# Where the rows lie in on-chip memory: token and key rows of a hybrid decoder layer alternate between two places modulo 256 bytes

## The chip, the core and the metric

The kernel runs on one core of one Trainium2 chip. A core has a matrix engine (TensorE; PE in the profile, with its weight loads listed apart as PEld), a vector engine (DVE), an activation engine (ACT), a general engine (POOL), a queue engine (SP), sixteen DMA engines, and an on-chip memory of 128 partitions that all engines read. Only TensorE multiplies matrices; its results go to accumulator banks that DVE and ACT read. The metric is the device time of one execution in microseconds (us). Differences of 0.2% (3 us here) are about what the runs can tell apart.

## The reference: what is computed

One layer of a decoder for 4,096 new tokens of one sequence and 64 tokens of eight others, model width 1,024, in float32:

```python
h = _rmsnorm(x, g_pre)
z = h @ w_in                                   # 1024 -> 2816 columns
cb, cc, ch, cg, q, k, v, ag, mq, mg = _split_cols(z)
out_a = silu(cg) * cb * conv3(cc * ch)         # gated convolution, 256 channels
out_b = silu(ag) * _window_prompt(q, k, v, sink)   # 8 heads, window 128
out_c = silu(mg) * _mem_attend(mq, mk, mv)     # 4 heads over 256 memory tokens
y = concat(out_a, out_b, out_c) @ w_out        # 1024 -> 1024
return x + _rmsnorm(y, g_post)
```

The keys and values of the memory tokens come from one more small projection of the memory rows.

## The kernel before

**Precision.** TensorE takes float32 operands in a one-pass form (`F32R` in the code) that keeps only the upper part of a number. Where that isn't enough an operand is split into `hi` (what the form keeps) and `lo` (the rest), and a product is the sum of three: weight hi by token hi, weight hi by token lo, weight lo by token hi. So most matmuls come in threes.

**Input projection** (`product`, the matmul at L373). Tokens go in 8 blocks of 520, a block as two halves of 260 columns. Blocks of weights and tokens are multiplied by Strassen's scheme in Winograd's form: seven products instead of eight (`PRODUCTS`), in three phases over groups of output columns (`PHASES`); the first two blocks of the first phase use the eight plain products. A product for one 128-wide group of outputs is twelve matmuls of 128x260: four slices k of the contraction, and for each the three of the split. The tokens stream through TensorE (the *moving* operand: row k of `hi` or `lo`, 260 numbers in each partition) against a loaded *stationary* operand (128 numbers in each partition, from a weight slot `w`, hi at `w[:, 0]` and lo at `w[:, 1]`). The order in a three is: hi against w-hi, lo against w-hi, hi against w-lo. There are 2x8x4x12 + (6x7x4 + 8x7x4 + 8x7x3)x12 = 7,488 such matmuls. `split` writes `hi` on ACT (L363) and `lo` on DVE (L364) one product ahead; DVE adds the results into the z tiles (L380).

**Attention and output projection.** Then, for each block of 128 tokens, 48 matmuls at L1499 (line `TE.matmul(acc, self.hl[l][:, k], wo[k]...)` in `Block.run`): 8 slices k, two halves of 512 columns, threes again. Here the 512 output weights `wo` are the moving operand, and the split attention result `mh` (hi) and `ml` (lo) the stationary one. 30 blocks run all 48 so with 512 columns, one more 24 (and 48 of 256 columns instead of the other 24), the block of the 64 sampled tokens 32 with a tile `mh_s`: 1,512 matmuls of 512 columns with `mh` or `ml`, and 32 with `mh_s`. Between them stand the matmuls of attention for a later chunk of 256 tokens: scores of the window (L1253, moving keys `kst`, hi part then lo part, against stationary queries `q`; 512 of 256 columns), scores of the memory (L1189, moving memory keys `mk` against `q`; 256 of 256 columns), transposes (L1204, L1276, L1153, moving the unit matrix) and the float32 sums with the values (L1095, L1225, L1231). `Block.split` makes `mh` on ACT (L1479) and `ml` on DVE (L1480).

**What sets the order.** In the plain blocks and the first phase the order on every engine is the program's. Later a list scheduler orders each engine's instructions by its own estimates, under the dependencies and the buffers: a tile of a pool can only be written when the pool's buffer is free again. The addresses come from the pools: these are laid out one behind the other on the left and right side of a partition, each as large as its tiles, so a pool that grows moves all behind it.

**Places.** The lines that set them: `wa = tile_pool(name="wa", bufs=3 * NP_)` (21 slots of 4,096 bytes: weights in the projection, then `wo`, `mh`, `ml` and the gain of the last norm), `wb` with 7 more, `hp` with two buffers for each of `hi` and `lo`, rows of `XR = 320` numbers (1,280 bytes) of which 260 are used, starting at number 48 (`hi`) or 16 (`lo`).

Of the kernel before, what the change touches and what calls it, by code (L numbers as in the profile page):

```python
# [8 lines left out]
F32 = mybir.dt.float32  # L9
F32R = mybir.dt.float32r  # L10
# [5 lines left out]
P = 128  # L16
D = 1024
KT = D // P
KH = KT // 2
# [2 lines left out]
NB = 8  # L22
NT = 4096 + NS
HW = 260
XR = 320
NBLK = NT // (2 * HW)
CT = 256
NCH = 4096 // CT
# [13 lines left out]
NP_ = len(PRODUCTS)  # L42
# [10 lines left out]
def hybrid_layer(ctx: ExitStack, tc: tile.TileContext, a: dict):  # L53
# [27 lines left out]

    wa = ctx.enter_context(tc.tile_pool(name="wa", bufs=3 * NP_))
    pa = ExitStack()
    wb_stack = ExitStack()
    wb = wb_stack.enter_context(tc.tile_pool(name="wb", bufs=NP_, side="right"))
# [1 line left out]

    place = ctx.enter_context(tc.tile_pool(name="place", bufs=1)).tile([P, 2, KH, HW], F32, name="place")  # L90
    hxp = pa.enter_context(tc.tile_pool(name="hx", bufs=4))
    hp = pa.enter_context(tc.tile_pool(name="hp", bufs=2))
    own = ExitStack()
    kept_z = ExitStack()
    zp, used = {}, {1: [], 2: []}
# [75 lines left out]
        return tp.tile([P, wide + 2 * HW], F32, tag="t", name=name)  # L171

    def w_slot(qi, name):
        return (wa if qi < 3 else wb).tile([P, 2, 512], F32R, tag="w", name=name)

    def w_raw(pair, o):

# [66 lines left out]
    nat, sq, after_nat = {}, [0], [14]  # L244
# [7 lines left out]
    def row_load(j):  # L252
        if j < 5 * NBLK:
            g = RG * j - NS
            if 2 <= j < 10 or 12 <= j < 14:
                t = (wa if j < 7 or j == 12 else wb).tile([P, 2, 512], F32, tag="w", name=f"nat{j}")
                t = nat[j] = t.rearrange("p a n -> p (a n)")
            else:
                t = nat[j] = natp.tile([P, D], F32, tag="nat", name=f"nat{j}")
            if g < 0:  # L260
                DMA.dma_start(t[:NS], a["x_s"])
                DMA.dma_start(t[NS:RG], a["x_p"][: RG - NS, :])
            else:
                DMA.dma_start(t[:RG], a["x_p"][g : g + RG, :])
# [86 lines left out]
                tc.keep_in_program_order(ins)  # L351
            store(hd[b][o], ops[o])

    begins = {"hi": 48, "lo": 16}

    def split_tile(tag, name):

        n = begins[tag]
        return hp.tile([P, KH, XR], F32R, tag=tag, name=name)[:, :, n : n + HW]

    def split(src, name):
        hi, lo = split_tile("hi", f"hi{name}"), split_tile("lo", f"lo{name}")
# [340 lines left out]
    x_of(0, 0, "B21")  # L703

    idle = accumulator(1, 2, "idle")
    warm = hp.tile([P, KH, XR], F32R, tag="lo", name="warm").rearrange("p k n -> p (k n)")
    G.memset(f(warm[:, : P + 512]), 1.0)
    for n in (416, 416, 416, 416, 512, 512, 512, 416):
        TE.matmul(idle[:, 0, :n], warm[:, :P], warm[:, P : P + n], start=True, stop=True)
# [19 lines left out]
    third = {}  # L729

    def third_start():
        keep = right.enter_context(tc.tile_pool(name="memkv", bufs=1, side="right"))
        third["mk"] = keep.tile([P, 2, 4, 256], F32R, name="mk")
        third["mkv"] = keep.tile([P, 2, 512], F32, name="mkv")

        third["vt"] = keep.tile([P, P], F32, name="vt")
        sink, nsink = (keep.tile([P, 8], F32, name=n) for n in ("sink", "nsink"))
        third["sink"], third["nsink"] = sink, nsink
        wmask = third["wmask"] = keep.tile([P, 2, P], U8, name="wmask")
        negs = third["negs"] = keep.tile([P, 2, P], F32, name="negs")  # L740
# [8 lines left out]
        third["mrows"] = third["pre"].tile([P, 4, P + CT], F32, tag="k", name="mrows").rearrange("p a n -> p (a n)")  # L749
# [262 lines left out]
    def open_attention():  # L1012

        nonlocal ps, mixp, places, vp, bp, bq, yp
        own.close()
        mem_stack.close()
        psa.close()
        pa.close()

        ps = {tag: ctx.enter_context(tc.tile_pool(name=f"ps{tag}", bufs=1 if tag == "pv" else 2, space=bass.MemoryType.PSUM))  # L1020
              for tag in ("s", "t", "z", "pv")}
        vp = ctx.enter_context(tc.tile_pool(name="vp", bufs=5, side="right"))
        yp = ctx.enter_context(tc.tile_pool(name="yp", bufs=2, side="right"))
# [12 lines left out]
        DMA.dma_start(third["scol"][:, 0:1], a["sinkcol"])  # L1036
# [60 lines left out]
    class Chunk:  # L1097
# [10 lines left out]
        def load_keys(self):  # L1108
            c, t0 = self.c, self.t0

            self.kst = self.pool("k").tile([P, 4, P + CT], F32R, tag="k", name=f"kst{c}")
            lo = P if c == 0 else 0
            if c == 0:
                G.memset(f(self.kst[:, :, 0:P]), 0.0)
            for kvh in range(2):
                for half in range(2):
                    G.dma_start(self.kst[half * 64 : half * 64 + 64, 2 * kvh : 2 * kvh + 2, lo:],  # L1117
                                  qd[:, 0, kvh * 64 : kvh * 64 + 64, t0 - P + lo : t0 + CT].rearrange("a p n -> p a n"))
            self.vT = self.pool("vT").tile([P, CT], F32, tag="vT", name=f"vT{c}")
            DMA.dma_start(self.vT, vd[:, self.ts])  # L1120
# [252 lines left out]

    def sample_window():
        zs = third["zs"]
        keys = bp["k"].tile([P, 4, P + CT], F32, tag="k", name="skc").rearrange("p a n -> p (a n)")
# [15 lines left out]
        values = third["pre"].tile([P, 4, P + CT], F32, tag="k", name="svc").rearrange("p a n -> p (a n)")  # L1392
# [63 lines left out]
    class Block:  # L1456
# [233 lines left out]
```

## Time and profile before

| what | value |
|---|---|
| median of 3 runs | 1530.43 us (1530.04 to 1531.11) |
| the profiled execution | 1529.03 us, of which 1527.3 us are the span from the first to the last instruction |
| TensorE (PE) busy | 1514.2 us, 99% of the span, 11,331 matmuls |
| weight loads (PEld) busy | 1391.6 us, 91% |
| DVE, ACT, POOL busy | 1145.1, 806.2, 381.0 us |
| granted TensorE clock | 1.000 of full speed |

Times in the profile's views are us from the span's start. A group's row has line, engine, operation, result<-operands, shape and count; then the time busy, the mean of one in ns, and the idle time before them. A matmul's duration reaches from its first column to its last result, so neighbours overlap, and what one matmul costs the engine is read from the distance between starts: in the timeline the first column is a row's start, the second its length, and `x2` says that two alike stand in it. The names of tiles are shortened: `hi_6T` is a `hi` tile, `w_2S` a weight slot, and digits that only number buffers are left out.

### The profile page before, as it was taken

The page shows a single profiled execution, that of the slowest core. Times are in us where ns is not written, and L with a number is a line of the kernel's source. Part 1 is how long each engine was busy: PE and PEld are TensorE (multiplying, and loading weights), DVE is VectorE, ACT ScalarE, POOL GpSimd, SP SyncE. Part 2 cuts the span into 40 slices and gives each one's busy share as a digit, 9 for nine tenths or more (in the row PEclk, how much of TensorE's full clock was granted, in tenths as well). Part 3 has the DMA queues.
Part 4 walks back from the last instruction along what each step waited for, and adds up shares of the span by engine and source line. Part 5 has one row for each costly group of instructions (what it writes and reads, how often), then busy time and mean ns, then how long its engine had stood idle before and what let it go on. Part 6 is the DMA issues. An engine that isn't in the chain of part 4 may idle for free.

```text
span 1527.3 us, 30150 instructions
## 1 busy us (share of the span) xinstructions
PE 1514.2 (99%) x11331; PEld 1391.6 (91%) x11331; DVE 1145.1 (75%) x2055; ACT 806.2 (53%) x2039; POOL 381.0 (25%) x604
## 2 busy tenths in 40 slices
PE   9999999999999999999999999999999999999998
PEld 9999999999999999999999998788888888888876
DVE  6778888899887777997677678766666666666743
ACT  7776666576222222445455457656655565565632
POOL 0222333221300000000101204544444444444310
PEclk9999999999999999999999999999999999999999
DMA  9989999878755333778877789977777777776333
GB/s 274 200 213 242 286 277 259 301 238 273 194 182 181 127 127 127 240 231 278 243 262 224 242 286 259 226 160 149 149 148 152 162 149 158 162 155 145 131 110 97
DMA packets 177943, 306.28 MB, mean 201 GB/s; under 512 B 33926, under 2 KB 107654, under 8 KB 177766
## 3 DMA queue, kind: packets, MB, share of 16 engines
q1 hardware_dynamic: 130901, 227.38, 48.2%
q0 software_dynamic: 46176, 75.92, 24.9%
q8 instruction: 90, 1.47, 0.4%
q10 hardware_dynamic: 720, 1.05, 0.2%
q14 instruction: 56, 0.45, 0.1%
HBM read 197.23 MB, written 108.05 MB: 200 GB/s over the span
## 4 chain that ended last, share of the span: by engine, by line
PE 87%; DVE 5%; issue 4%; DMA 2%; POOL 1%; ACT 1%; SPq 0%; ACTq 0%; POOLq 0%; DVEq 0%
PE c L373 47%; PE y L1499 23%; PE ws L1253 4%; PE wo L1095 2%; PE wt L1276 2%; PE xs L1189 2%; PE xt L1204 2%; PE wo L1225 2%; PE wo L1231 1%; PE mem_acc L796 1%; DVE z L380 1%; DMA ws10A<-in_w_in 1%; DMA vd<-v 1%; DMA place<-hd_B 0%; DMA ws20A<-in_w_in 0%
## 5 line engine op out<-in xcount | busy, mean ns | idle before, releaser
L1499 PE MATMUL y<-wo,mh 128*128 128x512 f32 (+1 forms) x1040 | 350.1, 399 | 0.0
L380 DVE TENSOR_TENSOR z<-c,z 128x520 f32<-128x520 f32 (+1 forms) x308 | 194.8, 647 | 80.7 <-PE c L373 79.0
L1499 PEld LDWEIGHTS y<-wo,mh 128*128 128x128 f32 x1040 | 194.3, 188 | 39.3 <-issue 2.4
L1499 PE MATMUL y<-wo,ml 128*128 128x512 f32 (+1 forms) x520 | 201.8, 388 | 0.0
L1266 ACT ACTIVATE sm<-sm,wnm 128x128 f32<-128x128 f32 x256 | 99.5, 390 | 60.9 <-DVE wnm L1260 60.0
L1198 POOL TENSOR_SCALAR xp<-xp,xrd 128x256 f32<-128x256 f32 x128 | 74.6, 590 | 208.0 <-DVE xrd L1194 207.1
L1499 PEld LDWEIGHTS y<-wo,ml 128*128 128x128 f32 x520 | 98.2, 189 | 16.2
L1190 DVE TENSOR_REDUCE xmx<-xs 128x2 f32<-128x512 f32 x64 | 44.1, 689 | 59.3 <-PE xs L1189 59.2
L1278 ACT COPY wpt<-wt 128x512 f32<-128x512 f32 x64 | 37.2, 582 | 87.7 <-PE wt L1276 85.2
L1253 PEld LDWEIGHTS ws<-kst,q 128*128 128x128 f32 x512 | 70.0, 190 | 5.4 <-ACT xp L1193 0.7
L1506 DVE TENSOR_TENSOR yn<-y,gpost 128x512 f32<-128x512 f32 (+1 forms) x66 | 45.1, 684 | 39.6 <-PE y L1499 39.3
L1253 PE MATMUL ws<-kst,q 128*128 128x256 f32 x512 | 73.1, 283 | 0.4 <-ACT xp L1193 0.4
L1507 ACT ACTIVATE y<-y 128x512 f32<-128x512 f32 (+1 forms) x66 | 38.5, 584 | 64.2 <-DVE yn L1506 64.2
L744 POOL CAST wmask<-negs 128x256 uint8<-128x256 f32 x1 | 0.8, 822 | 265.2 <-ACT z L382 265.2
L1286 POOL TENSOR_SCALAR_AFFINE_SELECT wpt<-wpt 128x512 f32<-128x512 f32 x64 | 52.7, 823 | 42.0 <-ACT wpt L1278 39.1
L1193 ACT ACTIVATE xp<-xs,xnm 128x256 f32<-128x256 f32 x128 | 58.9, 464 | 7.1 <-DVE xnm L1191 7.1
L1128 POOL DMA_DIRECT2D q<-qd x64 | 42.8, 674 | 70.2 <-DMA qd<-zh 60.2
L1117 POOL DMA_DIRECT2D kst<-qd x64 | 38.7, 617 | 63.7 <-PE xt L1204 41.5
L1517 DVE SCALAR_TENSOR_TENSOR xr<-yn,yst,xr 128x1024 f32<-128x1024 f32 (+2 forms) x34 | 43.1, 1269 | 14.6 <-POOL yst L1513 13.2
L1256 DVE COPY_PREDICATED sm<-wmask,ws 128x256 f32<-128x256 uint8 x124 | 52.1, 436 | 2.4 <-ACT sm L1255 2.0
L1283 POOL TENSOR_SCALAR_AFFINE_SELECT wpv<-wpt 128x512 f32<-128x512 f32 x62 | 40.5, 653 | 50.6 <-ACT wpt L1278 50.5
L275 ACT ACTIVATE nat<-nat 104x1024 f32<-104x1024 f32 x40 | 42.3, 1057 | 18.5 <-DMA nat<-in_x_p 18.5
(962 smaller groups left out, 5076.2 us busy)
## 6 DMA issues: line engine op xcount, KB each, us to landing
q<-qd POOLq DMA_DIRECT2D x64, 384.0 KB, 8.3
xr<-in_x_p SPq DMA_DIRECT2D x32, 512.0 KB
nat<-in_x_p SPq DMA_DIRECT2D x39, 416.0 KB
o_yp<-xr SPq DMA_DIRECT2D x31, 512.0 KB
md<-th POOLq DMA_DIRECT2D x48, 260.0 KB, 7.2
qd<-zh SPq DMA_DIRECT2D x48, 260.0 KB
qd<-z SPq DMA_DIRECT2D x48, 260.0 KB
kst<-qd POOLq DMA_DIRECT2D x60, 192.0 KB, 5.5
```

Source lines behind the costliest of these rows:

```text
L373: TE.matmul(bank[:, :HW], l, r, start=first and i == 0, stop=last and i == 3 * KH - 1)
L380: add = lambda dst, other: V.tensor_tensor(dst, c, other, op=ALU.add)
L1190: V.tensor_reduce(mx[:, :nb], s, axis=AX.X, op=ALU.max)
L1193: S.activation(p[:, i, :], s[:, i, :], AF.Exp, bias=nm[:, i : i + 1], scale=SCALE, accum_out=den[:, i : i + 1])
L1198: G.tensor_scalar(p[:, i, :], p[:, i, :], rd[:, i : i + 1], 0.5, op0=ALU.mult, op1=ALU.mult)
L1253: TE.matmul(s3[:, hh, :], self.q[:, 4 + 2 * (2 * half + hh) + kvh, i * P : i * P + P], self.kst[:, 2 * kvh + part, i * P : i * P + 2 * P], ...
L1256: V.copy_predicated(sm[:, 2 * half : 2 * half + 2, :], third["wmask"], third["negs"] if first else s3[:, :, 0:P])
L1266: S.activation(sm[:, hh, :], sm[:, hh, :], AF.Exp, bias=nm[:, hh : hh + 1], scale=SCALE, accum_out=den[:, hh : hh + 1])
L1286: G.affine_select(p3, p3, pattern=[[0, 4], [1, P]], compare_op=ALU.is_ge, fill=0.0, base=0, channel_multiplier=-1)
L1499: TE.matmul(acc, self.hl[l][:, k], wo[k][c0 // 512][:, r, c0 % 512 : c0 % 512 + c1 - c0], start=j == 0, stop=j == passes * KT - 1)
L1506: V.tensor_tensor(yn[:m, c0:c1], acc[:m], gpost[:m, c0:c1], op=ALU.mult)
L1517: V.scalar_tensor_tensor(self.xr[:m, cs], yn[:m, cs], st[:m, 3:4], self.xr[:m, cs], op0=ALU.mult, op1=ALU.add)
```

## The change

No instruction is added or removed: each engine has the same instructions as before. What changes is where tiles lie in a partition. Unused tiles (`pad`) are put between pools, rows get other lengths, `hi` and `lo` get a pool each, and four of the 21 slots of `wa` become a pool `wm` of their own, which holds four of the 28 weights of a phase (S3 of the column groups 0 and 1, A22 of 1 and 2) and later `mh` and `ml`. As the pools lay it out, the starts of the operands modulo 256 bytes are:

| operand | before | after |
|---|---|---|
| `hi`, row k, moving in L373 | 32 | 32 for even k, 160 for odd k (rows of 288 numbers) |
| `lo`, row k, moving in L373 | 160 | 160 for even k, 32 for odd k |
| weights, stationary in L373 | 224 | 224; 160 in the four slots of `wm` |
| `wo`, moving in L1499 | 224 | 224 |
| `mh`, `ml`, stationary in L1499 | 224 | 160 |
| `mh_s`, stationary in L1499 (sampled tokens) | 96 | 160 |
| `kst`, moving in L1253 | 96 or 160, hi and lo part alike | 160 hi part, 32 lo part (rows of 416 numbers) |
| `q`, stationary in L1253 and L1189 | the same place as `kst` | 96 |
| `mk`, moving in L1189 | 160, hi and lo part alike | 160 hi part, 32 lo part |
| unit matrix / what is transposed | 160 / 96 or 160 | 160 / 96 |
| float32 sums: moving / stationary | 96 / 160 | L1095 160 / 160, L1225 and L1231 96 / 96 |

"Moving minus stationary" below is the moving operand's place less the place of the stationary one that is loaded for the next matmul while it streams, modulo 256. It goes, in L373, from 64 for `hi` and 192 for `lo` to 64 and 192 by turns for either, so that the moving rows of successive matmuls lie at 32, 160, 32, 160 without a break (before: 32, 160, 32, 32, 160, 32); where the loaded weights lie in `wm`, to 128 and 0 by turns. In L1499 it goes from 0 to 64, in L1253 from 0 to 64 (hi part) and 192 (lo part).

The core of the diff:

```diff
-XR = 320
+XR = 288
+KR = 416
...
+    def pad(where, n):
+        pads[0] += 1
+        where.enter_context(tc.tile_pool(name=f"pad{pads[0]}", bufs=1)).tile([P, n], F32, name=f"pad{pads[0]}")
...
-    wa = ctx.enter_context(tc.tile_pool(name="wa", bufs=3 * NP_))
+    wa = ctx.enter_context(tc.tile_pool(name="wa", bufs=3 * NP_ - 4))
+    pad(ctx, 48)
+    wm = ctx.enter_context(tc.tile_pool(name="wm", bufs=4))
...
-    hp = pa.enter_context(tc.tile_pool(name="hp", bufs=2))
+    pad(pa, 32)
+    hp = {"lo": pa.enter_context(tc.tile_pool(name="hplo", bufs=2))}
+    pad(pa, 32)
+    hp["hi"] = pa.enter_context(tc.tile_pool(name="hphi", bufs=2))
...
     def w_slot(qi, name):
-        return (wa if qi < 3 else wb).tile([P, 2, 512], F32R, tag="w", name=name)
+        o = name[name.index("_") + 2 :]
+        pool = wm if (o, qi) in (("S3", 0), ("S3", 1), ("A22", 1), ("A22", 2)) else wa if qi < 3 else wb
+        return pool.tile([P, 2, 512], F32R, tag="w", name=name)
...
-    begins = {"hi": 48, "lo": 16}
-
     def split_tile(tag, name):
-        n = begins[tag]
-        return hp.tile([P, KH, XR], F32R, tag=tag, name=name)[:, :, n : n + HW]
+        return hp[tag].tile([P, KH, XR], F32R, tag=tag, name=name)[:, :, :HW]
...
-        third["mk"] = keep.tile([P, 2, 4, 256], F32R, name="mk")
+        third["mk"] = keep.tile([P, 2, 4 * 256 + 32], F32R, name="mk")[:, :, : 4 * 256].rearrange("p a (h k) -> p a h k", k=256)
...
+        pad(att, 16)
         bq = att.enter_context(tc.tile_pool(name="bq", bufs=1))
...
+        pad(att, 16)
         keys = att.enter_context(tc.tile_pool(name="keys", bufs=1))
...
-            self.kst = self.pool("k").tile([P, 4, P + CT], F32R, tag="k", name=f"kst{c}")
+            self.kst = self.pool("k").tile([P, 4, KR], F32R, tag="k", name=f"kst{c}")[:, :, : P + CT]
...
-            parts = lambda n: wa.tile([P, 2, 512], F32R, tag="w", name=n).rearrange("p a (b n) -> p (a b) n", n=P)
+            parts = lambda n: wm.tile([P, 2, 512], F32R, tag="w", name=n).rearrange("p a (b n) -> p (a b) n", n=P)
```

Since the slots of `wm` come free at other times than those of `wa` did, the scheduler's order differs at the seam between the projection and the output projection and for some blocks behind it; the order within L373 is the same throughout. Two places show it. On ACT, in the last products of the projection, the split of the output weights (`wo`, L181 before, L196 after), of the tokens (`hi`, L363 and L375) and of the first block's attention result (`mh`, L1479 and L1494). Before:

```order
L181 CAST wo_0_11673<-wor_11586 128x512
L363 CAST hi_7B_11710<-x_7B_11588 128x4x260
L181 CAST wo_0_11727<-wor_11645 128x512
L181 CAST wo_0_11730<-wor_11647 128x512
L181 CAST wo_0_11747<-wor_11649 128x512
L1479 CAST mh_11772<-place 128x1024
L363 CAST hi_7T_11776<-x_7T_11651 128x4x260
```

After:

```order
L196 CAST wo_0_11692<-wor_11605 128x512
L1494 CAST mh_11791<-place 128x1024
L375 CAST hi_7B_11729<-x_7B_11607 128x4x260
L196 CAST wo_0_11746<-wor_11664 128x512
L196 CAST wo_0_11749<-wor_11666 128x512
L196 CAST wo_0_11766<-wor_11668 128x512
L375 CAST hi_7T_11795<-x_7T_11670 128x4x260
```

The `mh` of block 0 moves ahead of one `hi` and three `wo`. On PE, in the second half of block 0's output projection (`y_1`), the scores of a window (`ws`, L1253 and L1268) of chunk 1. Before:

```order
L1499 MATMUL y_1_12155<-wo_1_11806,mh_11772 128x512
L1499 MATMUL y_1_12155<-wo_1_11806,ml_11773 128x512
L1499 MATMUL y_1_12155<-wo_1_11806,mh_11772 128x512
L1499 MATMUL y_1_12155<-wo_1_11823,mh_11772 128x512
L1499 MATMUL y_1_12155<-wo_1_11823,ml_11773 128x512
L1499 MATMUL y_1_12155<-wo_1_11823,mh_11772 128x512
L1253 MATMUL ws_1_0_12053<-kst_11254,q_11261 128x256 x4
L1253 MATMUL ws_1_1_12060<-kst_11254,q_11261 128x256 x4
```

After:

```order
L1514 MATMUL y_1_12185<-wo_1_11825,mh_11791 128x512
L1514 MATMUL y_1_12185<-wo_1_11825,ml_11792 128x512
L1268 MATMUL ws_1_0_12083<-kst_11273,q_11280 128x256 x4
L1268 MATMUL ws_1_1_12090<-kst_11273,q_11280 128x256 x4
L1514 MATMUL y_1_12185<-wo_1_11825,mh_11791 128x512
L1514 MATMUL y_1_12185<-wo_1_11842,mh_11791 128x512
```

The eight matmuls of the scores now stand behind two of the 24 of `y_1` instead of behind six.

More of the change, by code (lines that the diff above doesn't have):

```diff
@@ L79, in hybrid_layer @@
     md = tc.dram_tile([KT, P, NT], F32, name="md")
-    wa = ctx.enter_context(tc.tile_pool(name="wa", bufs=3 * NP_))
+    pads = [0]
+    def pad(where, n):
[4 more added lines that the diff above has]
+    wm = ctx.enter_context(tc.tile_pool(name="wm", bufs=4))
     pa = ExitStack()
@@ L255, in row_load @@
             if 2 <= j < 10 or 12 <= j < 14:
-                t = (wa if j < 7 or j == 12 else wb).tile([P, 2, 512], F32, tag="w", name=f"nat{j}")
+                t = (wm if j == 3 else wa if j < 7 or j == 12 else wb).tile([P, 2, 512], F32, tag="w", name=f"nat{j}")
                 t = nat[j] = t.rearrange("p a n -> p (a n)")
@@ L705, in hybrid_layer @@
     idle = accumulator(1, 2, "idle")
-    warm = hp.tile([P, KH, XR], F32R, tag="lo", name="warm").rearrange("p k n -> p (k n)")
+    warm = hp["lo"].tile([P, KH, XR], F32R, tag="lo", name="warm").rearrange("p k n -> p (k n)")
     G.memset(f(warm[:, : P + 512]), 1.0)
@@ L748, in third_start @@
         third["parts"] = third["pre"].tile([P, 12, CT], F32, tag="q", name="mparts").rearrange("p (a b) n -> p a (b n)", a=6)
-        third["mrows"] = third["pre"].tile([P, 4, P + CT], F32, tag="k", name="mrows").rearrange("p a n -> p (a n)")
+        third["pre"].tile([P, 16], F32, tag="pad", name="padk")
+        third["mrows"] = third["pre"].tile([P, 4, KR], F32, tag="k", name="mrows").rearrange("p a n -> p (a n)")
         third["mem"] = mem_stack.enter_context(tc.tile_pool(name="mem", bufs=3, side="right"))
@@ L1375, in sample_window @@
         zs = third["zs"]
-        keys = bp["k"].tile([P, 4, P + CT], F32, tag="k", name="skc").rearrange("p a n -> p (a n)")
+        keys = bp["k"].tile([P, 4, KR], F32, tag="k", name="skc").rearrange("p a n -> p (a n)")[:, : 4 * (P + CT)]
         kc = keys[:, : NB * P].rearrange("p (b k) -> p b k", b=NB)
@@ L1391, in sample_window @@
         yield
-        values = third["pre"].tile([P, 4, P + CT], F32, tag="k", name="svc").rearrange("p a n -> p (a n)")
+        values = third["pre"].tile([P, 4, KR], F32, tag="k", name="svc").rearrange("p a n -> p (a n)")[:, : 4 * (P + CT)]
         vc = values[:, : NB * P].rearrange("p (b k) -> p b k", b=NB)
```

## The prediction

> **What bounds the kernel.** I read the page first: busy shares, granted clock, chain.
>
> ```profile
> PE 1514.2 (99%) x11331; PEld 1391.6 (91%) x11331; DVE 1145.1 (75%) x2055; ACT 806.2 (53%) x2039; POOL 381.0 (25%) x604
> PEclk9999999999999999999999999999999999999999
> PE 87%; DVE 5%; issue 4%; DMA 2%; POOL 1%; ACT 1%; SPq 0%; ACTq 0%; POOLq 0%; DVEq 0%
> PE c L373 47%; PE y L1499 23%; PE ws L1253 4%; PE wo L1095 2%; PE wt L1276 2%; PE xs L1189 2%; PE xt L1204 2%; PE wo L1225 2%; PE wo L1231 1%; PE mem_acc L796 1%; DVE z L380 1%; DMA ws10A<-in_w_in 1%; DMA vd<-v 1%; DMA place<-hd_B 0%; DMA ws20A<-in_w_in 0%
> ```
>
> TensorE is busy in all 40 slices at its full clock, and 70% of the chain are two lines: the input projection (L373) and the output projection (L1499). Then the waits of PE, to see whether anything holds it:
>
> ```profile
> PE idle L709 <- POOL warm L707: 2.2, 1, 2.2
> PE c L373 <- DVE lo_2T L364: 0.9, 2, 0.5
> ```
>
> These are the two longest: nothing to gain there. No matmul is taken away either, so the change can only act on the pace at which matmuls follow each other. The pace comes from stretches in which PE does one thing only. First L373 in the stretch from 600 to 700 us, then its single starts in the timeline:
>
> ```profile
> 600.00:700.00 100.00, 100.00 (x851) 100.00 (x850) 1.00 0.72 239
> ```
>
> ```profile
> 600.01 0.28 PE L373 MATMUL c<-lo_6T,w_3S 128*128 128x260 f32 x1
> 600.13 0.40 PE L373 MATMUL c<-hi_6T,w_3S 128*128 128x260 f32 x2
> 600.37 0.28 PE L373 MATMUL c<-lo_6T,w_3S 128*128 128x260 f32 x1
> 600.48 0.40 PE L373 MATMUL c<-hi_6T,w_3S 128*128 128x260 f32 x2
> 600.72 0.28 PE L373 MATMUL c<-lo_6T,w_3S 128*128 128x260 f32 x1
> 600.84 0.40 PE L373 MATMUL c<-hi_6T,w_3S 128*128 128x260 f32 x2
> ...
> 602.13 0.28 PE L373 MATMUL c<-lo_6T,w_0S 128*128 128x260 f32 x1
> ```
>
> (851 overlap the stretch, some two of them only at its edges: 100 us / 849 = 117.8 ns.) From 600.01 to 602.13 stand six threes: 2.12 us / 6 = 353.3 ns, 117.8 each. Within a three the distances are unequal: after a `lo` 0.12, 0.11, 0.12 us, so 116 to 117; I take 116, which leaves (353.3 - 116) / 2 = 118.6 for a `hi`. Columns, stationary size and engine are the same, so something about `lo` is 2.6 ns cheaper. What differs by the table of places is that `lo` moves from 160 and `hi` from 32, 192 and 64 above the weights. The start of the kernel shows a second pace at the same places:
>
> ```profile
> 8.70 0.28 PE L373 MATMUL c<-lo_0B,w_1A 128*128 128x260 f32 x1
> ...
> 11.22 0.28 PE L373 MATMUL c<-lo_0B,w_3A 128*128 128x260 f32 x1
> ...
> 11.62 0.28 PE L373 MATMUL c<-lo_0B,w_3A 128*128 128x260 f32 x1
> ...
> 13.74 0.28 PE L373 MATMUL c<-lo_0B,w_0A 128*128 128x260 f32 x1
> ```
>
> Seven threes in 2.52 us are 360 ns each (120 a matmul); behind a short interruption at 11.3 six take 2.12 again. So the pace is one of several patterns that hold themselves. The output projection has the same: unsettled behind other matmuls, settled after some ten of its own.
>
> ```profile
> 1107.79 0.40 PE L1499 MATMUL y<-wo,ml 128*128 128x512 f32 x1
> ...
> 1110.11 0.40 PE L1499 MATMUL y<-wo,mh 128*128 128x512 f32 x1
> 1110.34 1.12 PE L1253 MATMUL ws<-kst,q 128*128 128x256 f32 x8
> 1111.30 0.60 PE L1204 MATMUL xt<-ident,xp 128*128 128x128 f32 x4
> ...
> 1495.00 0.39 PE L1499 MATMUL y<-wo,ml 128*128 128x512 f32 x1
> ...
> 1501.80 0.39 PE L1499 MATMUL y<-wo,ml 128*128 128x512 f32 x1
> ```
>
> The eleven from 1107.79 to 1110.34 take 231.8 ns each, the thirty from 1495.00 to 1501.80 take 226.7. The eight scores at 1110.34 take 120.0. One row shows L1499 at another place, 128 above its stationary operand, for the sampled tokens:
>
> ```profile
> L1499 PE MATMUL y<-wo,mh_s x32: 390/392/404, 1502.3 to 1509.5; 128*128 128x512 f32 x32
> ```
>
> 31 distances in 7.2 us are 232.3 ns, and it doesn't settle though nothing interrupts it. The settled sums have a common measure: 226.7, 120.0, 353.3 and 360 ns are 34, 18, 53 and 54 times 6.67 ns. I use that below as a guess at which paces can hold.
>
> **The change part by part.** The span's own execution took 1529.03 us, 1.4 below the median; the terms are differences to it and go to the median unchanged.
>
> *Product rows by turns.* 28 weights a phase, four in `wm`: S3 and A22 in two column groups are 2x2x12 matmuls in each of 22 Winograd blocks, A22 in two groups used twice in the two plain ones: 1,056 + 96 = 1,152. The other 6,336 keep weights at 224 while their rows go from two at 32 and one at 160 to half and half. At the two rows' prices a pair takes 118.6 + 116 = 234.6, 117.3 each: -0.5 ns, -2.9 us. If only multiples of 6.67 hold, the nearest pair is 35 times, 233.3 ns, 116.7 each: -1.1 ns, -7.0 us. I take the middle, -5.0. Ends: all rows as quick as `lo`, -1.8 ns on all 7,488, -13.3 us; all rows as in the first microseconds, 120.0, +2.2 ns, +16.6 us.
>
> *The 1,152 against `wm`* come to stand 128 and 0 above their weights. 0 is what the scores at 1110.34 had, at 120.0 for 256 columns; 128 is what `mh_s` had, 5.6 above the settled pace of the same line. I take 120: +2.2 x 1,152 = +2.6 us. Ends: 116, -2.1; 117.8 + 5.6, +6.5.
>
> *Output projection*, 1,512 matmuls from 0 to 64. About half stand within ten of an interruption, so today's mean is near (231.8 + 226.7) / 2 = 229.2. No row has 512 columns at 64; the nearest is the `hi` rows of L373, at 64, whose pattern is back within a three of the interruption at 11.3. I therefore take away the settling alone: 226.7, -2.5 x 1,512 = -3.8 us. Ends: one step of 6.67 below the settled pace, 220.0, -13.9; the pace of `mh_s`, 232.3, +4.7.
>
> *Keys*, 512 matmuls of 256 columns, from 0 to 64 and 192 by turns: now 120.0, afterwards what the product rows are taken at, 117.0, less four columns in 260, 115.2. Part of today's are quicker than 120, so I take -3.9, -2.0 us (ends -3 and +1).
>
> *What I cost at nothing.* The 256 scores against the memory already have 64 or 0 and change by 3.5 ns at most: 0.9 us either way. Transposes and float32 sums change place too; I have no row that shows a dependence, and bound both by 1 us. The order at the seam: block 0's split moves earlier, block 1's must wait for the last product that reads A22.
>
> ```profile
> 924.00:1010.00 86.00, 84.42 (x528) 1.00 1.03 234
> L1479 ACT CAST mh<-place x12: 1041/1047/1052, 913.0 to 1491.0; 128x1024 fp32r<-128x1024 f32 x12
> L1480 DVE TENSOR_TENSOR ml<-place,mh x12: 1218/1225/1241, 916.4 to 1492.1; 128x1024 fp32r<-128x1024 f32 x12
> ```
>
> PE idles 1.6 us in this stretch. Block 1's two splits take 1.05 + 1.23 = 2.3 us behind the product, under block 0's 48 matmuls (48 x 226.7 ns = 10.9 us). If that cover failed, the matmuls of block 1 and all behind them would be 2.3 us late. Queued behind the waiting split on ACT are the last conversions of keys and queries (`zh`), whose stores the second chunk's loads need. Together these count 0, within 3 us.
>
> Sum: -5.0 + 2.6 - 3.8 - 2.0 = -8.2 us: 1520.8 for a profiled execution, **1522.2 us** for the median.
>
> **The rivals.**
>
> *All rows at the quick pace.* If a `hi` is slow because the next or the last row lay at the same place (32 behind 32), alternation frees all 7,488: -13.3 - 3.8 - 2.0 = -19.1, 1511 us. For it: the pair 32, 32 is gone altogether. Against it: the two `hi` of a three take 0.24 together each time, and nothing in the rows sets the one before a `hi` apart from the one before a `lo`.
>
> *The place is not the cause.* `lo` is also always the middle one of three, the only one loaded with the same weights as its predecessor. If that makes it quick, nothing changes in L373, the output projection settles as before, and the time is 1530 us. The Trainium skill, "SBUF — State Buffer", section "SBUF: two separate sides", speaks for this: engine-side contention exists only on the port pair that the vector and general engines share, and "PE, ACT, and DVE's dedicated pair never wait on anyone". By that rule no place modulo 256 can cost TensorE anything. The trace neither confirms nor refutes it, since place and position in the three go together there; the two paces of L1499 (231.8 and 226.7) show at least that something beside the column count sets a matmul's cost.
>
> *Slower: the alternating rows hold the pattern of the first microseconds.* Its place is L373, its price 120.0 - 117.8 = 2.2 ns on 7,488 matmuls, +16.6, with the other terms as forecast -3.8 - 2.0: +10.8, 1541 us. For it: the pattern exists at these very places, and a pair has only the choice between 233.3 and 240 ns if multiples of 6.67 hold. Against it: it ended by itself at the first interruption and the stretch at 600 us shows the other. It decides from a mean pace of 117.8 + 5.8/7.488 = 118.6 ns.
>
> **How the numbers follow.** Forecast (small gain by place) 0.42, all rows quick 0.16, place not the cause 0.17, slower 0.25. What these runs can tell from no change is 0.2%, 3 us. Faster is the first two, 0.58; the same 0.17; slower 0.25. The forecast's own terms reach from about 1513 to 1528; all ends at once would give 1497 and 1556. For 8 in 10 I take 1504 to 1542, which holds the forecast, the quick rival, no change, and half of the slow one.
>
> **What would show it.** The stretch from 600 to 700 us with 854 to 859 matmuls of L373 instead of 851 bears out the first term; 835 is the slow rival, 851 the rule that place doesn't matter, 864 the quick rival. The distance behind `lo` and behind `hi` should depend on whether the row lies at 160 or at 32, so on k, and no more on the name. Rows against S3 and A22 of the moved slots should go at about 120. A stretch of L1499 behind an interruption should show 226.7 at once; more than 230 throughout would refute the third term, 220 would double it and more. The eight scores should take about 0.92 us instead of 0.96. If PE shows a new wait near the seam, what I costed at nothing was wrong.

## The result, and the profile after

The changed kernel takes 1541.04 us (median of 8 runs, 1537.97 to 1544.29) against 1531.03 us before (8 runs, 1530.04 to 1536.44). The ratio is 1.0062 (1.0051 to 1.0073): slower by about 10 us, where 8 us less was forecast. The profiled execution took 1539.86 us, with a span of 1538.2 us, 10.9 us more than before.

The page of the changed kernel: busy time of the engines, and the chain that ended last, by line.

```profile
PE 1525.7 (99%) x11331; PEld 1402.6 (91%) x11331; DVE 1146.4 (75%) x2055; ACT 807.5 (52%) x2039; POOL 382.2 (25%) x604
PEclk9999999999999999999999999999999999999999
PE c L385 54%; PE y L1514 23%; PE ws L1268 4%; PE wo L1110 2%; PE wt L1291 2%; PE xs L1204 2%; PE xt L1219 2%; PE wo L1240 2%; PE wo L1246 1%; DMA wr_1A<-in_w_in 1%; PE mem_acc L809 1%; DVE z L392 0%; DMA ws18A<-in_w_in 0%; DVE x_2T L362 0%; POOL xp L1213 0%
```

TensorE is busy 11.5 us longer with the same 11,331 matmuls, again at its full clock, and the weight loads with it (11.0 us); the other engines change by 1.3 us at most. (Lines stand 12 to 15 further down: the products are L385, the output projection L1514, the scores of the window L1268, the transposes L1219.) So the loss is one of pace. The next view gives TensorE's busy time and matmuls in a stretch, all lines together, for the kernel before:

```profile
0.00:924.00 924.00, 918.78 (x7674) 1.00 0.75 228
```

and after:

```profile
0.00:924.00 924.00, 920.07 (x7585) 1.00 0.75 227
```

By 924 us the changed kernel is 89 matmuls behind, at 117.9 ns each 10.5 us. That is nearly the whole loss, and it is made in the input projection. Its pace, from the timeline of the changed kernel (start, length, row):

```profile
599.98 0.28 PE L385 MATMUL c<-lo_6T,w_2S 128*128 128x260 f32 x1
...
601.40 0.28 PE L385 MATMUL c<-lo_6T,w_3S 128*128 128x260 f32 x1
...
602.84 0.28 PE L385 MATMUL c<-lo_6T,w_0S 128*128 128x260 f32 x1
```

From 599.98 to 601.40 stand four threes, 1.42 us, 118.3 ns a matmul; from 601.40 to 602.84 four more, 1.44 us, 120.0 ns. Before, six threes took 2.12 us, 117.8 ns a matmul, throughout. Over all distances between successive starts on L385 that are under 0.15 us (7,418 of them) the mean is 119.57 ns; before it was 117.90 ns on L373 (7,416). I call this mean the pace below.

Counted over six matmuls it becomes clearer. Before, 94% of the distances from a matmul to the sixth behind it are 707 ns (106 times 6.67 ns). After, 34% are 713 ns (107 times) and 60% are 720 ns (108 times), none 707.

What else moved, from the sums of the distances behind each kind of matmul (after less before, us):

| matmuls | change | made of |
|---|---|---|
| products, 7,488 | +10.8 | pace +1.67 ns x 7,418 = +12.4; distances over 0.15 us -1.8 (10.1 instead of 11.9) |
| output projection | +0.8 | pace of `mh`, `ml` 229.66 instead of 229.69 ns: nothing; the rest is waits between stages |
| scores of the window, 512 | -2.1 | pace 117.5 instead of 119.1 ns: -0.8; two waits behind them, 1.3 us together, are gone |
| transposes `xt` | +1.8 | new waits, next view |
| scores of the memory, 256 | -0.3 | pace 117.2 instead of 118.0 ns |
| sum of these | +11.0 | all matmuls together: +10.8 |

The waits of TensorE after, the longest sums behind the 2.2 us at the very start, which both kernels have:

```profile
PE xt L1219 <- POOL xp L1213: 1.9, 4, 1.1
PE c L385 <- DVE lo_0B L376: 0.5, 1, 0.5
```

The first is new: 1.9 us at the seam between the projections. It replaces waits of the same place before, which lay on `wt` and `ws`:

```profile
PE wt L1276 <- DVE xrd L1194: 0.9, 1, 0.9
PE ws L1253 <- ACT xp L1193: 0.4, 1, 0.4
```

The output projection and the scores after, again from the timeline:

```profile
1102.94 1.10 PE L1268 MATMUL ws<-kst,q 128*128 128x256 f32 x8
1103.88 0.60 PE L1219 MATMUL xt<-ident,xp 128*128 128x128 f32 x4
...
1495.55 0.39 PE L1514 MATMUL y<-wo,ml 128*128 128x512 f32 x1
...
1498.98 0.39 PE L1514 MATMUL y<-wo,ml 128*128 128x512 f32 x1
```

Eight scores take 0.94 us, 117.5 each. Fifteen distances of L1514 take 3.43 us, 228.7 each; before, in the same late stretch, they took 226.7. Behind an interruption the first four distances average 231.9 ns after and 232.5 ns before. So the line now starts a little quicker and settles higher, and the mean stays.

### The profile page after: what moved, and what is told of

Its sections match the earlier page's. It is cut to its first block, busy times and chain, and to the rows that moved or that the text cites. A ratio compares the mean times of both kernels' runs of the same rounds, so it can differ in the third digit from the quotient of the medians.

```text
span 1538.2 us, 30147 instructions
## 1 busy us (share of the span) xinstructions
PE 1525.7 (99%) x11331; PEld 1402.6 (91%) x11331; DVE 1146.4 (75%) x2055; ACT 807.5 (52%) x2039; POOL 382.2 (25%) x604
## 4 chain that ended last, share of the span: by engine, by line
PE 93%; DVE 3%; issue 1%; DMA 1%; ACT 1%; POOL 1%; ACTq 0%; SPq 0%; DVEq 0%; POOLq 0%
PE c L385 54%; PE y L1514 23%; PE ws L1268 4%; PE wo L1110 2%; PE wt L1291 2%; PE xs L1204 2%; PE xt L1219 2%; PE wo L1240 2%; PE wo L1246 1%; DMA wr_1A<-in_w_in 1%; PE mem_acc L809 1%; DVE z L392 0%; DMA ws18A<-in_w_in 0%; DVE x_2T L362 0%; POOL xp L1213 0%
## 5 line engine op out<-in xcount | busy, mean ns | idle before, releaser
L1514 PE MATMUL y<-wo,mh 128*128 128x512 f32 (+1 forms) x1040 | 350.9, 400 | 0.0
L1514 PEld LDWEIGHTS y<-wo,mh 128*128 128x128 f32 x1040 | 194.1, 188 | 39.0 <-issue 2.0
L1514 PE MATMUL y<-wo,ml 128*128 128x512 f32 (+1 forms) x520 | 201.6, 388 | 0.0
L1514 PEld LDWEIGHTS y<-wo,ml 128*128 128x128 f32 x520 | 98.2, 189 | 16.1
L1268 PEld LDWEIGHTS ws<-kst,q 128*128 128x128 f32 x512 | 69.3, 189 | 5.2 <-ACT xp L1208 0.3
L1268 PE MATMUL ws<-kst,q 128*128 128x256 f32 x512 | 71.9, 281 | 0.0
L394 ACT COPY z<-c 128x520 f32<-128x520 f32 (+1 forms) x44 | 24.4, 554 | 52.8 <-PE c L385 50.2
L1270 ACT COPY sm<-ws 128x256 f32<-128x256 f32 x128 | 44.4, 368 | 13.9 <-PE ws L1268 8.3
```

Of the source, the lines that this page charges most:

```text
L1268: TE.matmul(s3[:, hh, :], self.q[:, 4 + 2 * (2 * half + hh) + kvh, i * P : i * P + P], self.kst[:, 2 * kvh + part, i * P : i * P + 2 * P], ...
L1270: S.copy(sm[:, 2 * half : 2 * half + 2, :], s3[:, :, P : 2 * P])
L1514: TE.matmul(acc, self.hl[l][:, k], wo[k][c0 // 512][:, r, c0 % 512 : c0 % 512 + c1 - c0], start=j == 0, stop=j == passes * KT - 1)
```

## The experiments

In each, the rest is as in the kernel before. Where no range or ratio is given the time is that of one run; the median of before beside these runs was 1530.4 to 1530.6 us, its single runs up to 1536.6. The pace, over some 7,400 distances, tells more than a single time does.

**The two parts of the change apart.** First the product rows by turns alone, with all weights at 224 and nothing else moved.

```diff
-XR = 320
+XR = 288
-    hp = pa.enter_context(tc.tile_pool(name="hp", bufs=2))
+    pad(pa, 16)
+    hp = {"lo": pa.enter_context(tc.tile_pool(name="hplo", bufs=2))}
+    pad(pa, 32)
+    hp["hi"] = pa.enter_context(tc.tile_pool(name="hphi", bufs=2))
+    pad(pa, 16)
-        return hp.tile([P, KH, XR], F32R, tag=tag, name=name)[:, :, n : n + HW]
+        return hp[tag].tile([P, KH, XR], F32R, tag=tag, name=name)[:, :, :HW]
```

> The kernel before with the alternating product rows alone (hi and lo at 32 and 160 by turns; all weights stay at 224, keys, queries and output projection as before). Theory A, the alternating rows hold a slow pattern by themselves: a pace of 119.5 to 120 ns in the product line, six matmuls in 713 or 720 ns, +12 to +17 us, 1543 to 1548 us. Theory B, the slow pattern comes from the weights moved into the pool of their own: here they are not moved, so 116.7 to 117.8 ns, 1523 to 1531 us.

Measured: 1537.39 us (1535.95 to 1538.88), ratio 1.0042 (1.0027 to 1.0057), pace 119.22 ns; 69% of the sixes are 713 ns, 29% are 720. The rows by turns alone make most of the loss, and no moved weight is needed for it: theory A in kind, though pace and time stay below what it put.

Then the other half: the changed kernel with `hi` at 32 and `lo` at 160 for every k, as before (rows of 320 in one pool again).

```diff
-XR = 288
+XR = 320
-    hp = {"lo": pa.enter_context(tc.tile_pool(name="hplo", bufs=2))}
-    pad(pa, 32)
-    hp["hi"] = pa.enter_context(tc.tile_pool(name="hphi", bufs=2))
+    hp = pa.enter_context(tc.tile_pool(name="hp", bufs=2))
+    begins = {"hi": 0, "lo": 32}
```

> The changed kernel with the product rows as before (hi rows all at 32, lo rows all at 160, rows of 320 numbers), everything else of the change kept: moved weights, split attention result at 160, queries 64 below the keys, keys by turns. Theory A: 117.8 ns in the product line save for rows against moved weights at 119 to 120, keys cheaper by 2 us, output projection within 2 us of before: 1526 to 1532 us. Theory B: the product line stays at 119 to 120 ns, 1538 to 1542 us.

Measured: 1533.34 us, ratio 1.0017 (1.0004 to 1.0030), pace 118.31 ns. Against weights at 224 a row has the price of before (`hi` 118.5 and 119.2, `lo` 116.2 ns), against the four slots of `wm` 120.0 to 120.4. With 120.2 that is 2.3 ns on 1,152 matmuls, 2.6 us. The stretch from 100 to 700 us shows both halves, the products alone: with the rows by turns (first kernel)

```profile
100.00:700.00 600.00, 597.79 (x5000) 1.00 0.71 216
```

and with everything but them (second kernel):

```profile
100.00:700.00 600.00, 598.05 (x5048) 1.00 0.72 220
```

Before it was this row:

```profile
100.00:700.00 600.00, 597.07 (x5056) 1.00 0.72 221
```

56 matmuls fewer by the rows, 8 by the rest. The time is 1 us above what theory A put. The paces add: 117.90 + 1.32 + 0.41 = 119.63 ns, 119.57 measured with both.

**The keys alone.** Of the change only the places of keys, queries and memory keys (and of `mh_s`).

```diff
+KR = 416
-            self.kst = self.pool("k").tile([P, 4, P + CT], F32R, tag="k", name=f"kst{c}")
+            self.kst = self.pool("k").tile([P, 4, KR], F32R, tag="k", name=f"kst{c}")[:, :, : P + CT]
...
+        pad(att, 16)
```

> The kernel before with only the keys' side of the change: window keys by turns at 160 and 32, queries at 96, memory keys by turns, the pads that go with them; weights, product rows and split attention result as before. If the keys' part is a gain by itself, as the window scores of the two runs with it suggest (117.5 against 119.1 ns on 512 matmuls, 117.3 against 118.0 on 256): 1.0 us less, 1529.5 us, too little for the times to settle but plain in the pace of these lines. If the moved float32 operands or pads cost something, 1531 us or more.

Measured: 1529.24 us (12 runs), ratio 0.9993 (0.9980 to 1.0006): no difference that can be told. The scores go at 117.1 instead of 119.1 ns (2.0 x 512 = 1.0 us), the products at 117.90 as before. The output projection moves too: its 512-column matmuls with `mh` and `ml` go at 228.80 instead of 229.69 ns, though `wo`, `mh` and `ml` lie as before. With the keys moved as well and `mh`, `ml` at 160 (the second kernel) they go at 229.67.

**What the price of a row hangs on.** The next kernels change one line, the place of `hi` and of `lo` in a row of 320 numbers. The first exchanges them.

```diff
-    begins = {"hi": 48, "lo": 16}
+    begins = {"hi": 16, "lo": 48}
```

> The kernel before with the places of hi and lo exchanged: hi rows at 160, lo rows at 32, 2 of 3 matmuls now 192 above their weights. If the place of a row sets its cost: a hi 116, a lo 118.6, a three 350.6 or, in steps of 6.67, 346.7 ns; 1518 to 1524 us. If the position in the three does: a three 353.3, the middle one still the quick one, 1530 us. If a self-holding pattern of the sequence does, it can be 360: 1546 us.

Measured: one run of 1546.47 us, pace 120.70 ns. `hi`, now at 160, costs 121.6 and 123.0 ns, `lo`, now at 32, 117.6. In the timeline of this kernel ten threes take 3.62 us, 362 ns each:

```profile
601.05 0.28 PE L373 MATMUL c<-lo_6B,w_3A 128*128 128x260 f32 x1
...
604.67 0.28 PE L373 MATMUL c<-lo_6T,w_1S 128*128 128x260 f32 x1
```

So a row at 160 isn't quick by its place. The middle one of three stays the quicker one, but its neighbours pay for it. Now both names at one place, first 160:

```diff
-    begins = {"hi": 48, "lo": 16}
+    begins = {"hi": 16, "lo": 16}
```

> The kernel before with hi and lo rows both at 160, 192 above the weights, no change of place from matmul to matmul. If the place of a row sets its cost: 116 ns each or less (113.3 in steps), 1496 to 1518 us. If a change of place between successive rows is what makes a lo quick, or slow patterns come from successive rows at one place: 119 to 120 ns each, 1539 to 1547 us. If the position in the three does: 1530 us.

Measured: 1541.06 us, pace 120.01 ns; 98% of the sixes are 720. Four threes take 1.44 us:

```profile
599.88 0.28 PE L373 MATMUL c<-lo_6T,w_1S 128*128 128x260 f32 x1
...
601.32 0.28 PE L373 MATMUL c<-lo_6T,w_2S 128*128 128x260 f32 x1
```

Both at 32 (`begins = {"hi": 48, "lo": 48}`). The next expectations name two theories: by C the pace comes from how successive rows lie to each other, by D from how each lies to the weights that are loaded meanwhile.

> The kernel before with hi and lo rows both at 32, 64 above the weights. Theory C: 120.0 ns as with both at 160, since no row changes place: 1541 us. Theory D, with 64 and 192 not alike: another pace than 120.0, between 117 and 123 ns, 1524 to 1565 us.

Measured: 1542.87 us, pace 120.00 ns. The place that the quick rows of before have and the place that the slow ones have give the same pace when all rows lie there. At 32 `hi` and `lo` then cost the same (120.0 ns); at 160 it is `lo` that costs a little more (120.4 against 119.8). This is what theory C put; the next kernel speaks against it.

Both moved by 64 bytes, so that they keep their distance of 128 to each other and stand 128 and 0 above the weights (`begins = {"hi": 0, "lo": 32}`, places 96 and 224):

> The kernel before with both kinds of rows 64 bytes further on: hi at 96, lo at 224, still 128 apart, now 128 and 0 above the weights instead of 64 and 192. Theory C, the pace comes from how successive moving rows lie to each other alone (two at one place, one 128 off): a three stays at 353.3 ns, 1530 us. Theory D, it comes from how each lies to the weights that are loaded meanwhile: another pace, by the rows against moved weights of the run before about 360 or more, 1538 to 1548 us.

Measured: 1544.39 us, pace 120.42 ns. The distance between the two rows alone doesn't make the pace, so theory C falls. D put another pace than 120.0 for both rows at 32, so it doesn't hold as it stands either.

`hi` as before, `lo` 64 above it instead of 128 (`begins = {"hi": 48, "lo": 0}`):

> The kernel before with lo rows moved from 160 to 96, hi left at 32: 64 apart instead of 128, and 128 above the weights instead of 192. Theory C, it is the change of place that makes a lo quick: 353.3 ns if 64 will do as well as 128, 360 if not. Theory D, the quick matmul is the one 192 above its weights, and it is gone: 360 ns or more, 1541 us or more.

Measured: 1544.61 us, pace 120.04 ns.

The next kernel moves everything by 32 bytes, weights as well as rows, so that all operands but the unit matrix start at multiples of 64 and the differences between moving and stationary stay:

```diff
+    for side, n in (("left", 8), ("right", 56)):
+        ctx.enter_context(tc.tile_pool(name=f"pad_{side}", bufs=1, side=side)).tile([P, n], F32, name=f"pad_{side}")
```

> The kernel before with every pool 32 bytes further on (and the right side 224 bytes inwards), so that all operands of TensorE but the unit matrix start at a multiple of 64 bytes instead of 32 behind one; all differences modulo 256 between moving and stationary stay. If differences alone count: the same paces, 1530 us. If pieces of 64 bytes count, a row of 512 numbers touches 32 of them instead of 33: output projection at 220.0 ns settled instead of 226.7, scores 113.3 instead of 120, together about 10 to 14 us less, 1517 to 1520 us; the rows of 260 touch 17 either way.

Measured: 1531.86 us (10 runs), ratio 1.0002 (0.9992 to 1.0011), pace 117.89 ns. Six threes take 2.12 us, as before:

```profile
619.87 0.28 PE L375 MATMUL c<-lo_6T,w_3A 128*128 128x260 f32 x1
...
621.99 0.28 PE L375 MATMUL c<-lo_7B,w_0A 128*128 128x260 f32 x1
```

This common shift changes nothing, so the differences between the places count, and a start on a multiple of 64 is worth nothing here.

**Is there another arrangement as good?** The relation of before turned round (`hi` 0 and `lo` 128 above the weights, `begins = {"hi": 32, "lo": 0}`):

> The kernel before with hi rows at 224 and lo rows at 96: 0 and 128 above the weights, the reverse of the 128 and 0 that took 120.4 ns. If the pattern of before (hi 64, lo 192 above, 117.9 ns) is quick because lo lies 128 above hi in the ring of 256 and hi near the weights: about 118 ns, 1530 us. If only 64 and 192 in that order are quick: 120 to 121 ns, 1541 to 1549 us.

Measured: 1540.62 us, pace 119.99 ns. This is a mean of unequal parts: sixes take 711 to 729 ns, and only twelve matmuls make a steady 1,440 (96% of them).

`hi` as before at 64 above, `lo` at 0 (`begins = {"hi": 48, "lo": 32}`):

> The kernel before with lo rows moved from 160 to 224, level with the weights, hi left at 32. If it is enough that lo lies behind hi's place in the ring by 128 or more: below 119 ns, 1530 to 1538 us. If a lo is quick only at 192 above the weights: 120 ns, 1541 us or more.

Measured: 1543.53 us, pace 119.99 ns.

Both 32 bytes lower than before (`begins = {"hi": 40, "lo": 8}`):

> The kernel before with both kinds of rows 32 bytes earlier, hi at 0 and lo at 128: 32 and 160 above the weights, still 128 apart. If places count in steps of 64 bytes or the pattern is a broad one: 117 to 118.5 ns, 1526 to 1535 us. If it is a narrow one, 119 to 120.5 ns, 1538 to 1548 us.

Measured: 1544.54 us, pace 120.02 ns. 32 bytes beside the place of before, its whole advantage is gone.

`lo` as before, 192 above, and `hi` at 128 (`begins = {"hi": 0, "lo": 16}`):

> The kernel before with hi rows moved from 32 to 96, 128 above the weights, lo rows left at 160. If a lo 192 above the weights is quick wherever hi lies: 117 to 118.5 ns, 1524 to 1534 us. If both distances are needed: 120 ns, 1541 us or more.

Measured: 1551.62 us, pace 121.41 ns, the slowest of all. Eleven threes take 4.03 us, 366 ns each:

```profile
600.86 0.28 PE L373 MATMUL c<-lo_6B,w_1A 128*128 128x260 f32 x1
...
604.89 0.28 PE L373 MATMUL c<-lo_6T,w_0S 128*128 128x260 f32 x1
```

`lo` at its old place doesn't bring its old price along: it needs `hi` at 64.

**The succession.** Places as before, but for odd k the order in a three is lo, hi, hi.

```diff
-            for l, r in ((w[:, 0, ks], h[0][:, k]), (w[:, 0, ks], h[1][:, k]), (w[:, 1, ks], h[0][:, k])):
+            three = [(w[:, 0, ks], h[0][:, k]), (w[:, 0, ks], h[1][:, k]), (w[:, 1, ks], h[0][:, k])]
+            for l, r in (three if k % 2 == 0 else (three[1], three[0], three[2])):
```

> The kernel before with every place as before and another order in two of the four threes of a product: lo, hi, hi for odd k instead of hi, lo, hi. Six matmuls then go 32, 160, 32, 160, 32, 32 instead of 32, 160, 32, 32, 160, 32: more changes of place with the same rows at the same distance from the weights. If the quick pattern is bound to the distances alone: 117.9 ns, 1530 us. If it is bound to the repeated succession of two rows at one place and one at the other: 119 to 120 ns, 1538 to 1546 us.

Measured: 1538.57 us, pace 118.92 ns; 96% of the sixes are 713. In the timeline six sixes take 4.28 us:

```profile
620.29 0.28 PE L374 MATMUL c<-lo_6T,w_0A 128*128 128x260 f32 x1
...
624.57 0.28 PE L374 MATMUL c<-lo_6T,w_3A 128*128 128x260 f32 x1
```

No address differs from before, so the price isn't one of places alone either. The pace lies at the lower end of what the second reading put.

Only `hi` by turns (rows of 288), `lo` always at 160:

```diff
+ROW = {"hi": 288, "lo": 320}
...
+        return hp[tag].tile([P, KH, ROW[tag]], F32R, tag=tag, name=name)[:, :, :HW]
```

> Half of the row change: hi rows at 32 and 160 by turns, lo rows all at 160. Even k have the quick three of before, odd k have all three at 160 as in the run with both there. If threes keep their own price: (353.3 + 360) / 6 = 118.9 ns, 1538 us. If only an unbroken run of the quick three breaks 120: 119.5 to 120 ns, 1543 to 1547 us.

Measured: 1540.33 us, pace 119.86 ns; 52% of the sixes are 713, 40% over 721 ns.

Only `lo` by turns (`ROW = {"hi": 320, "lo": 288}`), `hi` always at 32:

> The other half: lo rows at 160 and 32 by turns, hi rows all at 32. Own prices: (353.3 + 360) / 6 = 118.9 ns, 1538 us. Unbroken run needed: 119.5 to 120 ns, 1543 to 1547 us.

Measured: 1535.46 us, pace 118.91 ns; 98% of the sixes are 713. Twelve threes take 4.28 us:

```profile
619.97 0.28 PE L382 MATMUL c<-lo_6T,w_2A 128*128 128x260 f32 x1
...
624.25 0.28 PE L382 MATMUL c<-lo_7B,w_1A 128*128 128x260 f32 x1
```

A three with `lo` at 160 takes some 353 ns, one with `lo` at 32 some 361. `lo` at its old place for half of the k keeps half of the advantage, as long as `hi` stays at 64. The two halves answer the same question differently: `lo` by turns comes out as if each three kept its own price, `hi` by turns does not (119.86 ns, in the range for "an unbroken run"). Neither reading holds for both.

**What follows.** Six arrangements (both at 160, both at 32, 64 apart, turned round, `lo` at 0, both 32 lower) have the pace 120.0 ns to within 0.04. I call it the ordinary pace of this line. It is 18 times 6.67 ns, with the relation turned round only as a mean. Before has the one pair of fixed places among those tried that goes below it: `hi` 64 and `lo` 192 above the weights that are loaded meanwhile, in the order hi, lo, hi. There each three saves one step of 6.67 ns, two in a six (720 - 707 = 13). With the other succession, or with `lo` by turns, one step in a six is left (713). With all rows by turns one step or none is left (713 or 720). Some arrangements cost more than the ordinary pace (120.4, 120.7 and 121.4). What the account of steps says is what was measured. Why a step is saved, and what the moving operand and the weight load share there, no run shows. Nor did I find why the rows by turns fall now into the one pattern and now into the other; in the kernel with them alone either one holds for over a thousand matmuls in a row.

## Why the prediction was wrong, step by step

**What bounds the kernel: right.** The loss is pace of TensorE on L385, with no other engine and no wait behind it, and most sixes of the products are multiples of 6.67 ns, as guessed. The forecast went the wrong way all the same. That 1541 us lies inside the stated range of 1504 to 1542 is owed to the slower rival, which the range took in by half, and not to the forecast's own terms, which ended at 1528.

**Product rows by turns: here it failed.** The step is "At the two rows' prices a pair takes 118.6 + 116 = 234.6, 117.3 each". It took the distances behind `lo` and `hi` for prices that belong to the places 160 and 32 and that go along when the places change hands. They belong to the whole pattern. With the places exchanged (`hi` at 160) the price at 160 was 121.6 to 123.0 instead of 116; with all rows at one place, either of the two, it was 120.0. On the 6,336 matmuls against weights at 224 the changed kernel has 119.5 ns (119.4 and 119.6), +1.6 x 6,336 = +10.1 us, where -5.0 was put. The second candidate, a pair of 35 steps (233.3 ns), never came up: six matmuls have 108 steps (720 ns) or 107 (713.3). I looked for the steps in pairs, and they lie in sixes.

**The 1,152 against `wm`: right in size.** +2.6 us forecast at 120 ns. With the other rows as before they took 120.2, +2.6 us; in the changed kernel 119.9 (119.2 and 120.6), +2.3 us. The 120 was taken from the scores, a line of 256 columns, and the price of `mh_s` stood against it; that the size came out is partly luck.

**Output projection: wrong, by 3.8 us.** "I therefore take away the settling alone" carried the behaviour of the 260-column `hi` rows over to 512 columns. The mean is 229.66 ns at 64 and 229.69 at 0. The distances still settle, and to 228.9 instead of 226.7 ns from the thirteenth on. The reading before was off as well: not half but 84% of the distances stand within ten of an interruption, since the line runs mostly in stretches of twelve (108 of them; only two are longer). From the fifth distance on they take 227 to 231 ns, so it is luck that the mean put for before, 229.2, is close. (31 blocks run all 48 of these matmuls, not the 30 named above; the count of 1,512 is right.) Nor is "nothing" the price of the moved `mh` and `ml` alone. The keys alone brought 229.69 down to 228.80, and with `mh` and `ml` moved too it is 229.67, so a loss of 0.9 ns (1.3 us) at 64 may cancel a gain that comes with the keys; no run moves `mh` and `ml` by themselves. The 32 matmuls of `mh_s` went from 232.6 at 128 to 228.8 ns at 64, a gain of 0.1 us.

**Keys: right in sign.** -2.0 us forecast with 3.9 ns a matmul; measured 1.6 ns, -0.8 us. It is the old pattern's price again that was carried over: eight scores take 0.94 us, not 0.92. The memory's scores gained 0.8 ns, 0.2 us, inside the 0.9 either way.

**What was costed at nothing.** The seam cost no more than the 3 us allowed. Transposes wait 1.9 us for `xp`, which was not named; the two waits that it replaces were 1.3 us. The products' own waits fell by 1.8 us. The block's split that was feared to be late shows no wait. The forecast's sign for trouble, a new wait near the seam, did show, but it is worth 0.6 us.

Sum of the terms as measured: +10.1 + 2.3 - 0.8 - 0.2 for the paces, -1.8 for the products' waits, together +9.6; the remaining 1.2 of the 10.8 us lie between stages (the output projection's +0.8, the seam's +0.6, small ones).

**The rivals.** The slower one had place, mechanism and time right: L385, the pattern of the first microseconds, 1541 us. Its price was a little high (120.0 on all, 119.57 measured), and its gains of 5.8 us elsewhere came to 1.0. Its threshold, a mean pace of 118.6 ns, was passed. What spoke for it in the text, that a pair can only choose between multiples, was the better reading; what I held against it, that this pattern "ended by itself at the first interruption", was true of the rows of before and said nothing of other rows. It was also half of what the same rows show: the pattern began at an interruption too (from 7.2 to 8.1 us the starts lie 118 ns apart, at 8.1 to 8.6 there is a gap, and 120 ns follow). So an interruption can start either pattern, and even before, 4% of the sixes are 720 ns. "All rows at the quick pace" is refuted by the rows by turns alone (119.22 ns). "The place is not the cause" is refuted as well: the kernels with both rows at 160 and both at 32 change nothing but addresses, and their pace is 120.0 instead of 117.9 ns, 2.1 x 7,488 = 15.7 us (their times, single ones, moved by 10.5 and 12.3 us). By that rival each of them would take 1530 us; one run of each took 1541.06 and 1542.87 us. The Trainium skill, "SBUF — State Buffer", section "SBUF: two separate sides", says that PE never waits on anyone, and says it of contention between engines. The prediction concluded from it that no place modulo 256 can cost TensorE anything. That conclusion fails here; the rule itself no run tests, for both operands are TensorE's own.

**The checks named.** The stretch from 600 to 700 us holds 836 matmuls instead of 851: the slow rival's mark (835), not the forecast's 854 to 859. That the distance should depend on the place and no more on the name fell too: behind rows at 32 it is 119.4 ns, behind rows at 160 119.6. L1514 behind an interruption showed 231.9, not 226.7, "at once".

## What to carry to other kernels

A price that is read from single rows of a settled sequence belongs to the sequence, and it isn't additive: before adding such prices over another order or other places, run the sequence itself, and read its pace from start distances over six or twelve matmuls. Where a line is already below the pace that its neighbours in shape have (here 117.9 against 120.0 ns, which the kernel's own first microseconds showed), a change of addresses or order has more to lose than to gain: of the thirteen other arrangements and orders of these rows that ran, none was quicker. Moving a tile for quite another purpose can cost as much as this change did: 32 bytes were enough for 2.1 ns on each of 7,488 matmuls.

## What the hardware showed that was not expected

With columns, weights, order and dependences unchanged, start addresses alone moved the pace of a split 128x260 matmul between 117.9 and 121.4 ns (1530 to 1552 us for the kernel). A common shift of weights and rows by 32 bytes changes nothing (ratio 1.0002, 0.9992 to 1.0011), a shift of the rows alone by 32 bytes costs everything (120.02 ns). The order of the three matmuls counts as well at unchanged addresses (118.92 ns). And in most arrangements the time comes in steps: sixes are 106, 107 or 108 times 6.67 ns, and those of the slowest arrangement 108 or 110 times (720 and 733 ns). It is not so in all: with the rows exchanged, turned round or moved by 64 bytes the sixes spread over many lengths between 710 and 733 ns.
